# The last store of a DMA-bound RMSNorm kernel, cut into six transfers with uneven shares per DMA engine

## The chip, the cores and the metric

One core of a Trainium2 chip runs the kernel alone. The metric is device time in microseconds (us) per execution. Sixteen DMA engines (the number over which the page takes its shares) move the data between HBM, where the input and output lie (67.12 MB read and 67.11 MB written by the page), and SBUF, the core's own memory, in which a tile here has 128 partitions. SP, ACT, DVE and POOL are the core's SyncE, ScalarE, VectorE and GpSimd engines. All runs quoted here were classed as fast; there were no slow ones to set aside. Before the change the kernel took 320.66 us (median of 3 runs, 320.62 to 321.44).

## The reference

```python
x: (8, 1024, 2048) float32;  gamma: (2048,);  eps = 1e-5
rms = np.sqrt(np.mean(x ** 2, axis=-1, keepdims=True) + eps)
out = gamma * x / rms
return (out * (1 / (1 + np.exp(-out)))).astype(np.float32)
```

The input has 67 MB and so has the output. There is little arithmetic per byte.

## The kernel before

The 8192 rows are handled in 16 blocks of 512. A block is one tile of 128 partitions, four rows of x side by side in each, so a partition holds 32 KB that are contiguous in memory. Below, "a row" is such a 32 KB row of a block. Loads and stores are issued from SP, each as one transfer of 128 rows.

```python
J = 4
BUFS, LEAD = 6, 5
xb = x2.rearrange("(b p j) d -> b p (j d)", p=P, j=J)
ob = o2.rearrange("(b p j) d -> b p (j d)", p=P, j=J)
...
def load(b):
    xt = pool.tile([P, J * d], f32, name="xt")
    nc.sync.dma_start(out=xt, in_=xb[b])
    blocks[b] = xt
...
def finish(b):
    for j in range(J):
        nc.vector.scalar_tensor_tensor(...)          # x * rstd * gamma, in place
        if j % 2:
            ...
            nc.scalar.activation(out=pair, in_=pair, func=ACT.Silu)
    nc.sync.dma_start(out=ob[b], in_=blocks.pop(b))
    del rstds[b]
...
    nc.scalar.dma_start(out=grow[0:1, 0:d], in_=...gamma...)   # the only transfer of one row
    for b in range(LEAD):
        load(b)
    ...
    for b in range(nblk):
        if b + 1 < nblk:
            stats(b + 1)
        finish(b)
        if b + LEAD < nblk:
            load(b + LEAD)
```

## Time and profile before

| | before |
|---|---|
| time, median | 320.66 us |
| span of the profiled run | 319.4 us |
| mean DMA rate over the span | 420 GB/s |
| ACT busy / DVE busy | 67% / 57% |
| last compute ends | 293.9 us |

The page's third part shows where the DMA time goes: per queue, its packets, megabytes and the share of 16 engines' span that its packets took.

```profile
q1 hardware_dynamic: 4608, 134.22, 98.1%
q10 hardware_dynamic: 2, 0.01, 0.0%
```

One queue, SP's, carries everything and fills 98.1% of what sixteen engines could do in the span. The packet count is 4096 rows (16 loads and 16 stores of 128) and 512 completion packets, 16 for each of the 32 transfers; in the trace they have 4 bytes and take 0.009 us. Queue q10 is gamma's row and its completion packet. The engines stand idle only in the other 1.9%, and most of that is the tail.

### The profile page before, as it was taken

What the parts mean: (1) busy time and instruction counts of PE and PEld (TensorE: products, weight loads), DVE (VectorE), ACT (ScalarE), POOL (GpSimd) and SP (SyncE); (2) the same over time, 40 slices, a digit from 0 to 9 for tenths busy, and PEclk for the clock granted to TensorE, in tenths of its full rate; (3) what the DMA queues carried; (4) which work ended last, traced back from release to release, by engine and by line L of the source; (5) the groups of instructions that cost most, each with busy time, mean ns of one, the idle gap of its engine ahead of it and who ended that gap; (6) DMA issues with size and microseconds to landing.
All of it is one profiled execution on the core that took longest, in us unless ns stands there. A gap on an engine that the chain in (4) does not pass through costs nothing.

```text
span 319.4 us, 433 instructions
## 1 busy us (share of the span) xinstructions
DVE 181.7 (57%) x96; ACT 213.1 (67%) x130; POOL 58.4 (18%) x38
## 2 busy tenths in 40 slices
DVE  0209998897629185390854909449093672993000
ACT  1249999999968478484784748747487674876000
POOL 0203232511304004040030402204021040400000
DMA  8999999999999999999999999999999999999992
GB/s 325 427 415 456 410 447 386 410 447 415 439 443 420 439 423 435 447 411 447 419 435 439 419 456 415 439 431 427 439 427 435 439 423 439 431 431 443 415 447 123
DMA packets 4612, 134.24 MB, mean 420 GB/s; under 512 B 513, under 2 KB 513, under 8 KB 513
## 3 DMA queue, kind: packets, MB, share of 16 engines
q1 hardware_dynamic: 4608, 134.22, 98.1%
q10 hardware_dynamic: 2, 0.01, 0.0%
q14 instruction: 2, 0.02, 0.0%
HBM read 67.12 MB, written 67.11 MB: 420 GB/s over the span
## 4 chain that ended last, share of the span: by engine, by line
DMA 75%; DVE 8%; ACT 5%; issue 3%; DVEq 1%; SPq 1%; ACTq 0%
DMA out_dram<-xt 59%; DMA xt<-in_x_dram 16%; DVE xt L74 8%; ACT xt L78 3%; ACT junk_a L63 3%; DVEq L127 1%; SPq L49 1%; DVE ss L59 0%; DVE junk_v L59 0%; ACTq L63 0%; DVEq L74 0%; DVEq L59 0%; SPq L79 0%
## 5 line engine op out<-in xcount | busy, mean ns | idle before, releaser
L74 DVE SCALAR_TENSOR_TENSOR xt<-xt,rstd,g 128x2048 f32<-128x2048 f32 x64 | 146.1, 2346 | 2.2 <-POOL rstd L69 2.2
L63 ACT ACTIVATE junk_a<-xt 128x2048 f32<-128x2048 f32 x48 | 90.2, 1880 | 60.0 <-DMA xt<-in_x_dram 59.0
L78 ACT ACTIVATE xt<-xt 128x4096 f32<-128x4096 f32 x32 | 115.2, 3613 | 19.5 <-DVE xt L74 19.5
L59 DVE CUSTOM_DVE_ANT_0 junk_v<-xt 128x2048 f32<-128x2048 f32 x16 | 36.8, 2299 | 106.3 <-DMA xt<-in_x_dram 106.3
L66 POOL TENSOR_SCALAR var<-ss 128x4 f32<-128x4 f32 x16 | 17.8, 1114 | 210.0 <-ACT junk_a L63 199.3
L69 POOL TENSOR_TENSOR rstd<-var,half 128x4 f32<-128x4 f32 x16 | 38.0, 2376 | 1.3
L63 ACT ACTIVATION_READ_ACCUMULATOR junk_a<-xt 128x1 f32 x48 | 8.9, 186 | 0.0
L89 POOL PARTITION_BROADCAST g<-xt x1 | 2.3, 2302 | 9.5 <-issue 9.5
L59 DVE DVE_READ_ACCUMULATOR2_ANT ss<- 128x1 f32 x16 | 2.3, 141 | 0.0
L63 ACT ACT_TABLE_LOAD x1 | 1.3, 1283 | 1.3 <-PEq L113 1.3
L78 ACT ACT_TABLE_LOAD x1 | 1.3, 1283 | 0.0
L88 POOL MEMSET half<- 128x4 f32 x1 | 0.1, 101 | 0.3 <-POOLq L113 0.3
L113 POOL MEMSET const-float32-0.0<- 128x1 f32 x1 | 0.1, 98 | 0.2 <-issue 0.2
L113 POOL MEMSET const-bfloat16-1.0<- 128x1 bf16 x1 | 0.1, 101 | 0.0
L113 POOL MEMSET const-uint8-127<- 128x1 uint8 x1 | 0.1, 101 | 0.0
L113 POOL MEMSET const-float32-1.0<- 128x1 f32 x1 | 0.1, 98 | 0.0
## 6 DMA issues: line engine op xcount, KB each, us to landing
xt<-in_x_dram SPq DMA_DIRECT2D x16, 4096.0 KB, 29.4
out_dram<-xt SPq DMA_DIRECT2D x16, 4096.0 KB, 38.3
xt<-in_gamma_dram ACTq DMA_DIRECT2D x1, 8.0 KB
```

Source lines behind the costliest of these rows:

```text
L49: nc.sync.dma_start(out=xt, in_=xb[b])
L59: nc.vector.tensor_tensor_reduce(out=junk_v, in0=row(b, j), in1=row(b, j), scale=1.0, scalar=0.0, op0=ALU.mult, op1=ALU.add, accum_out=ss[ ...
L63: nc.scalar.activation(out=junk_a, in_=row(b, j), func=ACT.Square, accum_out=ss[:, j:j + 1])
L66: nc.gpsimd.tensor_scalar(out=var, in0=ss, scalar1=1.0 / d, scalar2=float(eps), op0=ALU.mult, op1=ALU.add)
L69: nc.gpsimd.tensor_tensor(out=rstd, in0=var, in1=half, op=ALU.pow)
L74: nc.vector.scalar_tensor_tensor(out=row(b, j), in0=row(b, j), scalar=rstds[b][:, j:j + 1], in1=g, op0=ALU.mult, op1=ALU.mult)
L78: nc.scalar.activation(out=pair, in_=pair, func=ACT.Silu)
L88: nc.gpsimd.memset(half, -0.5)
L89: nc.gpsimd.partition_broadcast(g, grow[0:1, 0:d])
L113: nc = _bacc.Bacc("TRN2", target_bir_lowering=False, num_devices=1)
L127: with _tile.TileContext(nc) as tc:
```

## The change

The last store leaves some engines idle at its end (from 313 to 316 us a quarter of them are busy, a DMA share of 0.25), because four engines run late (their last rows end at 316.4 to 317.8 us, those of the other twelve at 313.1 to 314.0). The change means to even this out by uneven shares.

```diff
-        nc.sync.dma_start(out=ob[b], in_=blocks.pop(b))
+        xt = blocks.pop(b)
+        parts = [(0, P, 0, J)]
+        if b == nblk - 1:
+            parts = [(0, 112, 0, 4), (112, 120, 0, 3), (112, 120, 3, 4), (120, 124, 0, 2),
+                     (120, 124, 2, 4), (124, 128, 0, 4)]
+        for p0, p1, j0, j1 in parts:
+            nc.sync.dma_start(out=ob[b, p0:p1, j0 * d:j1 * d], in_=xt[p0:p1, j0 * d:j1 * d])
         del rstds[b]
```

## The prediction

k is the number of engines that a transfer goes to, and the numbers of engines are labels, which no trace shows. 0 stands for gamma's engine, 0 to 3 for the four engines that carry the 16 KB packets of the changed kernel, and 0 to 7 for the eight that carry its 24 KB packets. How the rows would be dealt was assumed; the trace of the changed kernel then showed it (seven rows of 32 KB on all sixteen engines, one packet of 24 and one of 8 KB on eight, two of 16 KB and one of 32 KB on four of these). "Ports bind" names the case that engines which read neighbouring partitions at one time slow each other.

The forecast's sum was +2.4 us for two more rows on late engines and at most +10.9 for slowed rows in the three small parts, if the four late engines went through these in step, so at worst +13.3; between these the author chose about +9, which gives 329.7 us.

> **What bounds the kernel now.** I read the page first, for which engine is full. Parts 2 and 6:
>
> ```profile
> DMA  8999999999999999999999999999999999999992
> GB/s 325 427 415 456 410 447 386 410 447 415 439 443 420 439 423 435 447 411 447 419 435 439 419 456 415 439 431 427 439 427 435 439 423 439 431 431 443 415 447 123
> ...
> xt<-in_x_dram SPq DMA_DIRECT2D x16, 4096.0 KB, 29.4
> out_dram<-xt SPq DMA_DIRECT2D x16, 4096.0 KB, 38.3
> ```
>
> The DMA engines are over 90% busy in every slice but the first and the last. Nothing else is: ACT, the busiest compute engine, has 67%. Only the last slice (8 us) has room, so next came the end: the timeline, the waits of the issuing queue, and busy time in stretches (columns of the last: stretch, its length, DVE, ACT and POOL busy us, TensorE clock, DMA share, GB/s).
>
> ```profile
> 290.29 3.62 ACT L78 ACTIVATE xt<-xt 128x4096 f32<-128x4096 f32 x1 [0.91 <-DVE xt L74]
> 293.93 0.33 SPq L79 DMA_DIRECT2D out_dram<-xt  x1
> ```
>
> ```profile
> SPq L127 <- DMA out_dram<-xt: 23.7, 1, 23.7
> ```
>
> ```profile
> 280.00:303.00 23.00, 10.26 (x5) 11.19 (x4) 0.00 (x0) 1.00 1.00 433
> 303.00:313.00 10.00, 0.00 (x0) 0.00 (x0) 0.00 (x0) 1.00 0.99 429
> 313.00:316.00 3.00, 0.00 (x0) 0.00 (x0) 0.00 (x0) 1.00 0.25 109
> 316.00:319.40 3.40, 0.00 (x0) 0.00 (x0) 0.00 (x0) 1.00 0.02 10
> ```
>
> Compute is over at 293.9 and the last store is issued at once. It then queues behind earlier transfers until about 303, and everything that follows is DMA. From 313 to 316 the share is 0.25: a quarter of the engines still work and the rest have run dry. That is the imbalance that the change can touch.
>
> The packet records of the same trace show it by engine. They do not name the engine, but packets on one engine follow each other within nanoseconds, so I linked them into sixteen chains. A row of a block is one packet of 32,768 bytes; its usual duration is 1.213 us and the next starts 1.21 us later (27.1 GB/s, times 16 = 433, as the stretch says). Time after the span's start at which each chain's last row ends:
>
> ```
> twelve chains   313.1 to 314.0 us
> four chains     316.4, 316.7, 316.8, 317.8 us
> ```
>
> The twelve carry about 1.3 to 1.9 us of packet time over 1.213 each in the whole run, nearly all before 53 us. The four carry 4.5 to 5.9 us, and they go on stalling, at about the same moments (near 150, 170 and 208 us, for example). So four engines lag by some three rows, and the slowest sets the end: it finishes at 317.8, the queue sees it at 318.1, and the span ends at 319.4.
>
> Which four? Gamma's row is the only transfer that uses one engine. Its completion packet ends 2.454 us after the span's start, and the first row on one of the four lagging chains starts 0.003 us earlier, exactly the overlap seen after every other completion packet. So gamma's engine is a laggard.
>
> [...] row durations keep to 1.213 us, with no two engines seen halving each other.
>
> **The change part by part.** It removes one store of 128 rows, 8 rows on each engine, and adds six on the same queue. The built program keeps the same order of everything else; the extra issues wait on nothing that is not long done. [...]in rows of 32 KB:
> - 112 rows, k = 16: 7 on every engine.
> - 8 rows of 24 KB and 8 rows of 8 KB, k = 8: 0.75 + 0.25 on engines 0 to 7.
> - 4 rows of 16 KB twice and 4 rows of 32 KB, k = 4: 0.5 + 0.5 + 1 on engines 0 to 3.
>
> Engines 0 to 3 thus get 10 rows (before 8), engines 4 to 7 get 8, engines 8 to 15 get 7; 40 + 32 + 56 = 128.
>
> Issuing: six at about 0.33 us (the row above) is 2 us, over at 296, while the engines reach this store at about 303. Hidden. Completion packets: five more at 0.009 us, nothing.
>
> Rows, each engine alone: two more on engines 0 to 3 is 2 x 1.21 = 2.42 us. If they are the laggards, the end moves from 317.8 to 320.2: +2.4 us. If only engine 0 of them lags (316.8), 316.8 + 2.4 = 319.2 and the end moves by +1.4. Fast engines with ten rows end at 314 + 2.4 = 316.4 at most, below the old end.
>
> [...] the four lagging chains enter the last store at 306.7, 307.0, 307.1 and 308.1[...]. [...] The 112-row part adds a smaller loss[...]. The four come within 1.4 us of each other[...], so I choose a value nearer to being in step: about +9 us.
>
> **The rivals.** First: no port binds, an engine's own 1.21 us per row does. Then +1.4 to +2.4, about 323. [...] Second: the lower eight are not the laggards. If all laggards are in 8 to 15, the slowest loses one row, 1.21 us, and the time is 319.4; further gain is impossible because it still has seven rows. For it: that is the change's evident intent. Against: the chain that follows gamma. Third: rows are dealt by partition number whatever the shape; then each engine has eight rows again and the time stays 320.7. [...] Fourth: the six issues delay the start; against it, the engines have 9 us of queue left when they are issued.
>
> Even perfect balance gives little: the mean of the chains' ends is near 314.3, 3.5 us or 1.1% before the end, so over 2% faster is out of reach.
>
> **Range and chances.** Ports bind: 65%, about 329.7 (from 326 to 335). They do not, and the laggards are low: 28%, about 323. No loss or a small gain: 7%, 319.4 to 320.7. The middle of this is near 328. Over 2% slower means above 327.1, which the first case passes nearly nine times in ten: 0.65 x 0.88 = 0.57. Faster by 2%: 0.01. The rest, 0.42, is within 2%. Range 321.5 to 335.
>
> **What would show it.** Rows of the last store over 1.213 us[...] show ports binding; all at 1.213 refutes it. The final stretch should show about four engines (a share near 0.25) for 10 us or more; a share of 0.25 for some 5 us says rows alone. The final wait of the issuing queue should grow from 23.7 to about 31 us, since the last store's first issue comes at the same time and six issues take 2 us of it. An end before 317 with the four chains one row shorter would show the laggards in the upper half, and my reading of gamma's engine wrong.

The overlap of 0.003 us by which the text follows gamma's engine holds for most completion packets rather than for every one: in this trace 405 of the 512 of SP's queue have a row that starts 0.003 us before their end, and 49 more one at 0.004. And "row durations keep to 1.213 us" is, counted: of the 3441 rows that start after 53 us, 3375 took at most 1.22, and the longest 2.11.

## The result, and the profile after

The changed kernel took 331.79 us (median of 4 runs, 331.64 to 332.9) against 320.92 for the kernel before (4 runs). The six parts cover the block exactly once, but the record has no check of this run's result. The ratio is 1.0345, with a 95% interval of 1.0317 to 1.0372: slower by over 2%. A ratio is the mean time of one kernel's fast runs over that of the other's of the same rounds, so it is not quite the ratio of the medians quoted.

Parts 2 and 6 of the page of the changed kernel, the lines that answer to those of before:

```profile
DMA  8999999999999999999999999999999999999931
GB/s 318 443 424 431 420 420 380 439 435 435 420 421 431 443 435 428 428 428 431 443 420 439 431 424 420 439 443 428 424 428 435 439 431 439 428 428 424 301 110 33
...
out_dram<-xt SPq DMA_DIRECT2D x15, 4096.0 KB, 33.2
out_dram<-xt SPq DMA_DIRECT2D x1, 3584.0 KB
out_dram<-xt SPq DMA_DIRECT2D x1, 192.0 KB
out_dram<-xt SPq DMA_DIRECT2D x3, 64.0 KB
out_dram<-xt SPq DMA_DIRECT2D x1, 128.0 KB
```

Up to the thirty-seventh slice nothing has changed. In the thirty-eighth the DMA digit is still 9 while the rate has fallen from some 430 to 301 GB/s. Engines that count as busy and move less have packets that take longer (of the 135 rows that start after 303.3 us, 28 took over 1.8 times the usual 1.213 us). That is a different picture from engines that have run out of work, as from 313 to 316 us before, where the share fell to 0.25 and the rate with it, to 109 GB/s.

The timeline at the end, and the last wait of the issuing queue:

```profile
291.16 3.62 ACT L78 ACTIVATE xt<-xt 128x4096 f32<-128x4096 f32 x1 [0.91 <-DVE xt L74]
294.80 5.01 SPq L85 DMA_DIRECT2D out_dram<-xt  x6
```

```profile
SPq L133 <- DMA out_dram<-xt: 29.9, 3, 27.1
```

Compute ends at 294.8, less than 1 us later than before. The six issues take 5.0 us, over at 299.8, while the first engine reaches this store at 303.8: hidden. The wait at the end, 23.7 us before, is 29.9 in total. Busy time in stretches:

```profile
303.00:313.00 10.00, 0.00 (x0) 0.00 (x0) 0.00 (x0) 1.00 1.00 341
313.00:316.00 3.00, 0.00 (x0) 0.00 (x0) 0.00 (x0) 1.00 0.73 208
316.00:319.40 3.40, 0.00 (x0) 0.00 (x0) 0.00 (x0) 1.00 0.38 145
319.40:325.00 5.60, 0.00 (x0) 0.00 (x0) 0.00 (x0) 1.00 0.22 53
325.00:331.10 6.10, 0.00 (x0) 0.00 (x0) 0.00 (x0) 1.00 0.09 27
```

From 303 to 313 the share is 1.00 and the rate 341 GB/s; before, the share was 0.99 and the rate 429. From 319.4 to 325 a share of 0.22, between three and four engines, moves only 53 GB/s; as many undisturbed ones would move 0.22 x 433 = 95, an estimate from the 433 GB/s at a share of 1.00 from 280 to 303. (These lines count a packet wholly in the stretch where it starts, so a share can also pass 1.)

I linked the packets of this trace into sixteen chains as in the prediction. Each last part tells which engine class a chain is: 16 KB packets go to four engines, 24 KB packets to eight. Times are us after the span's start: entry into the last store, end of the seven rows, and end of the last packet.

```
eight chains, seven rows only      enter 304.0 to 307.0   end 312.6 to 317.8
four chains, + 24 KB + 8 KB        enter 303.8 to 304.5   end 316.1 to 319.7
four chains, + 24 + 8 + 16 + 16 + 32 KB:
    enters 308.97   seven rows to 320.46   last packet to 325.22
    enters 309.28   seven rows to 321.16   last packet to 327.02
    enters 308.20   seven rows to 320.55   last packet to 328.82
    enters 309.58   seven rows to 321.68   last packet to 329.47
```

The four engines that got ten rows are exactly the four that come latest to this store. (Of the first eight, two came at 306.9 and 307.0, after a last row of 2.1 us in the store before, and the others by 304.4.) Gamma's completion packet again runs into one of those four chains with an overlap of 0.003 us. Of the 135 rows of 32 KB that start after 303.3 us, 28 take more than 1.8 times the usual 1.213 us, the longest 3.36; before, all 139 in that stretch took 1.213 us.

For the slowest chain the sum is this (us). The last row ended at 317.79 before and at 329.47 after, +11.68. It entered the last store at 309.58 instead of 308.12, +1.46. Its seven rows took 12.10 instead of 7 x 1.21 = 8.47, +3.63. Its last three rows' worth took 7.78 instead of 3.63, +4.15. Two rows more than before are +2.42. Together: 11.66. The slowest chain need not be the same engine in both runs: in the trace before it was not gamma's, which ended at 316.77. The late entry is again a row that takes long: its last row of the store before took 2.46 instead of 1.21, while the fast engines were already at the 112-row part. That store is one whole transfer of 128 rows, and before the change the same rows all kept 1.21; so I put the loss down to what the other engines do at that time. (The profiled run, 332.9 us, was the slowest of the four. By medians the change costs 10.9.)

### The profile page after: what moved, and what is told of

Its sections match the earlier page's. It is cut to its first block, busy times and chain, and to the rows that moved or that the text cites. A ratio compares the mean times of both kernels' runs of the same rounds, so it can differ in the third digit from the quotient of the medians.

```text
span 331.1 us, 438 instructions
## 1 busy us (share of the span) xinstructions
DVE 181.9 (55%) x96; ACT 213.1 (64%) x130; POOL 60.1 (18%) x38
## 4 chain that ended last, share of the span: by engine, by line
DMA 72%; DVE 7%; ACT 5%; issue 3%; DVEq 1%; SPq 1%; POOL 0%; ACTq 0%; POOLq 0%
DMA out_dram<-xt 56%; DMA xt<-in_x_dram 16%; DVE xt L74 7%; ACT xt L78 3%; ACT junk_a L63 2%; DVEq L133 1%; SPq L49 1%; POOL rstd L69 0%; DVE ss L59 0%; DVE junk_v L59 0%; DVEq L74 0%; ACTq L63 0%; DVEq L59 0%; SPq L85 0%; POOLq L66 0%
## 5 line engine op out<-in xcount | busy, mean ns | idle before, releaser
L66 POOL TENSOR_SCALAR var<-ss 128x4 f32<-128x4 f32 x16 | 19.5, 1220 | 209.2 <-ACT junk_a L63 197.3
```

What stands on the lines that cost most here:

```text
L66: nc.gpsimd.tensor_scalar(out=var, in0=ss, scalar1=1.0 / d, scalar2=float(eps), op0=ALU.mult, op1=ALU.add)
```

## The experiments

My theory is that the change costs time in two ways: two more rows on the four late engines, 2.4 us, and engines that now read neighbouring partitions of SBUF at one time and slow each other, the rest. The expectations call the second "Ports", and engines that slow each other so "share". No trace names a port or an engine. The rivals are that rows alone count (any further cost lying elsewhere), that the number of transfers or the small transfers on few engines cost time, and that the source partitions have no part in it. Six kernels were run with three rounds each; the kernel before took 320.69 us in the rounds of the first four and 320.99 in those of the last two, which ran on another chip. The diffs are cut to the lines that matter; those of the run from the change's partitions and of the upper-first run are against the experiment before.

**The 112-row part alone.** The eighth row's worth goes out as a column strip of all 128 rows, to a spare tensor, so engines stay even. Rows 112 to 127 of the last block are not written; the result is wrong.

```diff
-        nc.sync.dma_start(out=ob[b], in_=blocks.pop(b))
+            nc.sync.dma_start(out=ob[b, 0:112], in_=xt[0:112])              # last block only
+            nc.sync.dma_start(out=spare[:, 0:1024], in_=xt[:, 0:1024])
```

> The last block's store is the change's 112-row part, followed by one eighth of the columns of all 128 rows written to a spare tensor, so every engine still moves eight rows' worth and the second part is dealt as the full store was. Rows 112 to 127 of the last block are not written: a wrong result on purpose. Ports (my theory): [...]rows of this part double to about 2.4 us in many places, the lagging engines also finish the store before it later (in the changed kernel by 1.5 us) and their seven rows take 12.1 us instead of 8.5; the end moves by +4 to +6 us, time about 326. Rival (only the row counts and the extra transfers count): counts are equal, so within 0.5 us of before, 321.

It took 325.95 us (325.74 to 326.28), ratio 1.0166 (1.015 to 1.0181): +5.3 us with equal work on every engine. Of the 121 rows of 32 KB that start after 303.3 us, 21 take over 1.8 times 1.213 us. Busy time in stretches, to compare with 0.99 and 429 GB/s, then 0.25 and 109, in the prediction:

```profile
303.00:313.00 10.00, 0.00 (x0) 0.00 (x0) 0.00 (x0) 1.00 1.01 353
313.00:316.00 3.00, 0.00 (x0) 0.00 (x0) 0.00 (x0) 1.00 0.68 212
```

So the 112-row part costs about half of the change by itself, before any engine has more to do than another. Why its rows double was not shown, and which rows each engine gets was not seen.

**The five small transfers from spread partitions.** The last store stays whole; behind it go five transfers of the change's sizes, read from every fourth partition.

```diff
+            # (first row of spare, (first partition, rows, partition step), columns in blocks of d)
+            for r0, src, j0, j1 in [(112, (0, 8, 4), 0, 3), (112, (0, 8, 4), 3, 4), (120, (32, 4, 4), 0, 2),
+                                    (120, (32, 4, 4), 2, 4), (124, (1, 4, 4), 0, 4)]:
+                nc.sync.dma_start(out=spare[...], in_=xt[...])
```

> The last store stays one transfer of 128 rows; behind it go five extra transfers to a spare tensor, with the sizes and engine counts of the change's five small ones, but read from every fourth partition[...]. Engines 0 to 3 move 11 rows, 4 to 7 nine, 8 to 15 eight. Both theories: three more rows on the four lagging engines, 3 x 1.21 = 3.6 us, all packets at their usual rate (24 KB in 0.91, 16 KB in 0.61, 8 KB in 0.31 us); time about 324.5 (324 to 325.2). If small transfers on few engines had a cost of their own, or if the engines 0 to 3 were not the laggards (then about 321.3), it would show here.

It took 324.54 us (324.33 to 324.73), ratio 1.0121 (1.0105 to 1.0136): +3.85. Three more rows are 3.63 us.

**The same five from the change's partitions.** Only the source partitions differ.

```diff
-            [(112, (0, 8, 4), 0, 3), (112, (0, 8, 4), 3, 4), (120, (32, 4, 4), 0, 2),
-             (120, (32, 4, 4), 2, 4), (124, (1, 4, 4), 0, 4)]
+            [(112, (112, 8, 1), 0, 3), (112, (112, 8, 1), 3, 4), (120, (120, 4, 1), 0, 2),
+             (120, (120, 4, 1), 2, 4), (124, (124, 4, 1), 0, 4)]
```

> As e2_own_ports, but the five extra transfers read the partitions that the change reads (112 to 119, 120 to 123, 124 to 127)[...]. Same sizes, same engines, same destination rows. Ports: the tail costs the lagging engines 7 to 9 us instead of 3.6 (7.8 in the changed kernel), with 24 KB packets up to 3 us; time about 328.5 (327.5 to 331). Rival (only rows count): the same as e2_own_ports, about 324.5.

It took 329.0 us (328.51 to 329.63), ratio 1.0259 (1.0238 to 1.0279). The pair is the clearest: same instructions, sizes, engines and destination rows, and 4.5 us between them. Busy time in stretches, first from spread partitions:

```profile
313.00:316.00 3.00, 0.00 (x0) 0.00 (x0) 0.00 (x0) 1.00 0.33 142
316.00:319.40 3.40, 0.00 (x0) 0.00 (x0) 0.00 (x0) 1.00 0.25 106
```

and from the change's partitions:

```profile
313.00:316.00 3.00, 0.00 (x0) 0.00 (x0) 0.00 (x0) 1.00 0.54 150
316.00:319.40 3.40, 0.00 (x0) 0.00 (x0) 0.00 (x0) 1.00 0.22 43
```

From 316 to 319.4 both have nearly the same share of busy engines, 0.25 and 0.22, and one moves 106 GB/s, the other 43. The packets agree. There are eight of each size; the shortest and the longest:

```
spread:         24 KB  0.91 to 0.91 us    16 KB  0.61 to 0.61    8 KB  0.31 to 0.31
the change's:   24 KB  1.09 to 2.72 us    16 KB  0.61 to 2.41    8 KB  0.57 to 1.45
```

The 16 KB packets are again carried by the four late chains, and by no others, in both runs. From the change's partitions their last five packets take 5.0, 6.8, 8.9 and 8.7 us, from spread ones 3.7. The pair shows that the source partitions decide; what it is that engines on neighbouring partitions share was not shown.

**Two halves by partition.** Equal rows and only two transfers, but each is read from 64 partitions instead of 128.

```diff
-        parts = [(0, P)]
+        parts = [(0, P)] if b < nblk - 1 else [(0, 64), (64, P)]
```

> The last store as two transfers of 64 rows, partitions 0 to 63 and 64 to 127, four rows on each engine in each: equal rows, two transfers[...]. Ports: rows of the last store take about 2.4 us; for two fast engines that share, sixteen row times from 303.5, to about 323, which is +5; time 326 (325 to 329). Rival (only rows count): 321.

It took 331.19 us (330.35 to 331.89), ratio 1.0327 (1.0306 to 1.0348): the sign and the row times as the theory says (a median of 2.52 us for the 142 rows that start after 303.3, 94 of them over 1.8 times the usual), the sum twice my +5 and outside the range. The loss is +10.5 us for one store of 4 MB. I had overlooked that the late engines still had three rows of the store before to read, and now supposed that the lower half slows these.

**The halves in the other order**, to test that.

```diff
-        parts = [(0, P)] if b < nblk - 1 else [(0, 64), (64, P)]
+        parts = [(0, P)] if b < nblk - 1 else [(64, P), (0, 64)]
```

> The two halves of e4_halves in the other order: partitions 64 to 127 first, then 0 to 63. e4_halves took 5 us more than I expected. My explanation: in its first half [...]the lagging engines still had three rows of the store before[...]. With the upper half first those leftover rows are not disturbed, the lagging engines' partners run alone for some 4 us, and the end is set by two fast engines that share throughout: 303.5 + 16 x 1.21 = 322.9 for the last row against 317.8, +5; time about 326 (324.5 to 327.5). If the order did not matter: 331, as e4_halves.

It took 328.48 us (327.95 to 329.73), ratio 1.0238 (1.02 to 1.0277), so +7.5 against the kernel before of its own rounds, where the lower half first cost +10.5. The order matters, but my number was missed: 326 was expected, 327.5 at most. The late engines' leftover rows keep their 1.21 us here, and no row of the last store takes over 2.78, where the run before had rows of up to 4.93. The twelve fast engines end at 321.3 to 322.5 (expected 322.9). But the end is set by the late four, at 324.2 to 326.3. I had paired each late engine with a fast one. The trace says otherwise: the fast engines already took 2.56 us a row while the late ones were still on the store before, and the late engines' rows doubled when they arrived. One of them entered at 308.2, took seven of its eight rows at 2.1 to 2.6 us, and came to 326.3 in this way. I infer that fast engines slowed fast ones here and late engines late ones; which rows each engine gets in a 64-row transfer was not seen.

**Six transfers by columns.** Each is read from all 128 partitions, as the whole store was.

```diff
+        cuts = [0, J * d]
+        if b == nblk - 1:
+            cuts = [0, 4096, 5120, 6144, 7168, 7680, 8192]
+        for c0, c1 in zip(cuts, cuts[1:]):
+            nc.sync.dma_start(out=ob[b, :, c0:c1], in_=xt[:, c0:c1])
```

> The last store as six transfers again, but cut by columns: each has all 128 rows[...]. Both theories that count rows or ports: within 0.7 us of before, about 321[...]. If the number of transfers itself cost the time in the change, up to +10 us.

It took 320.98 us (320.49 to 321.54), ratio 1.0003 (0.9963 to 1.0042). Six transfers in place of one cost nothing that these runs can see; every packet of 16, 4 and 2 KB took 0.611, 0.159 and 0.084 us. With the run from spread partitions (its packets of 24, 16 and 8 KB took no longer than 0.91, 0.61 and 0.31), this rules out the number and the smallness of the transfers as the cause here.

No version came out that beats the kernel before. In these runs a transfer on fewer than sixteen engines went each time to engines that include the late ones (the 16 KB packets to just these four, the 24 and 8 KB packets to these and four more), so it added to them. Giving the late engines fewer rows than the others was not tried.

## Why the prediction was right

**What bounds the kernel, and that four engines set the end:** right. From 53 to 280 us and from 280 to 303 us the DMA rate was 432 and 433 GB/s before, 431 and 433 after; the only other rows slowed were the last ones of the store before, on the chains that came late. (Of the moments that the prediction names for stalls, the slowest chain has none near 150 us.)

**Gamma's engine is late, so the change loads the wrong engines:** right. The chains with 16 KB packets were the late four in the changed kernel and again in both runs with five extra transfers. The trace before showed this for gamma's chain alone; that the other three belong to the same set of four was left open ("If they are the laggards") and came true without having been read from a trace. Four late chains stand in all eight traces, on two chips at least (in the kernel before with 4.5 to 5.9 us of packet time over the usual, against 1.3 to 1.9 for the others); why they lag stays open. The change took rows off eight engines that had some 3 us to spare and put two on each of the four that had none. That term was predicted at +2.4 us, and the run from spread partitions measures its rate: +3.85 for three rows, 1.28 each.

**Ports bind:** right in what can be seen, that engines slow each other by the partitions that they read, and it was the branch held at 65%. The pair of runs that differ in source partitions alone shows 4.5 us. That a port is the cause was the author's estimate and not shown.

**Its size:** about +9 was said for this branch and +10.9 came, 331.8 against 329.7; the stated middle, 328, mixed in the branches that failed. The step that was mis-sized is "The 112-row part adds a smaller loss". It is not the smaller one. Alone it costs 5.3 us, in the changed kernel's slowest chain 3.63 on its seven rows and about 1.2 on the last row of the store before, which the prediction did not think of. The three small parts went the other way. The author's estimate gave them up to 10.9 us more than their rows; they cost 4.15. The late engines enter up to 1.4 us apart (308.20 to 309.58), which may have kept them out of each other's way; that is a guess, not measured. Two errors of opposite sign left the sum nearly right, and that is luck.

**Issuing:** "six at about 0.33 us" was 5.0 us in all instead of 2. It was hidden, as said, with some 4 us to spare.

**What would show it:** slow rows in the small parts came, up to 2.94 us for 24 KB, which took 0.91 at best. The final wait was to grow to about 31 us and is 29.9. "A share near 0.25 for 10 us or more" came only in part: 0.22 from 319.4 to 325, then 0.09, because the four chains end apart, from 325.2 to 329.5.

The rivals fell: rows alone (324.5 even with eleven of them, by the run from spread partitions), laggards in the upper half (the chains), and an even deal by partition number (one 24 KB packet on each of eight chains).

## What to carry to other kernels

Before giving engines uneven work, find out which ones are late; a transfer seen to run on one engine, followed into the next packet's start, can point to one, as gamma's did with an overlap of 0.003 us. When a transfer is cut, cut it by columns and keep all 128 partitions in each piece: that was free here (ratio 1.0003), while cuts by partition cost 5 to 11 us in one store (+5.3 for the 112-row part alone, +7.5 and +10.5 for the halves, +10.9 for the change). In these runs, a share of busy engines that stayed up while the rate fell (1.00 at 341 GB/s) went with engines that slowed each other, and a share that fell with its rate (0.25 at 109 GB/s) with engines that had run dry.
